# Attention products on all 128 rows: rests of the keys beside zeros, decay and compressed values stacked in parts

## The chip, the cores and the metric

The kernel runs on one core of a Trainium2 chip. The metric is the time of one execution on the device in microseconds. A core has five engines with a queue each: TensorE (PE; its weight loads are shown apart as PEld), VectorE (DVE), ScalarE (ACT), GpSimd (POOL) and SyncE (SP), which issues the transfers.

## The reference

Two blocks of two layers each work on 256 tokens of width 1024 (the first block also on 256 tokens of context). Everything is float32. Cut to what the change touches, in the second block:

```
# forgetting attention: c is the cumulated log of a gate
logits = einsum('bhqd,bhkd->bhqk', q, k) * scale + c[..., q] - c[..., k]
p = softmax(where(k <= q, logits, -inf));  o = p @ v
# compressed, selected and window attention
p_c = masked_softmax(q @ kc + rel, c_end <= t);  o_c = p_c @ vc      # 15 compressed blocks per group
o_s = masked_softmax(q @ k_slc + rel) @ v_slc
o_w = masked_softmax(q @ k_win + rel) @ v_win
out = g0 * o_c + g1 * o_s + g2 * o_w
```

A third attention has a sliding window of 128 with a sink. The first block has two attentions over 512 keys (256 of x and 256 of the context), one of them with a bias per head and one with a window and a sink. Heads have 64 features, and there are 8 heads in each attention.

## The kernel before

Every float32 product is made of products of a faster type. A number is split into a part that this type (float32r) holds exactly and its rest: `mm3` issues part x part, part x rest and rest x part (L546 to L548). Nearly all projections run through it, with weights streamed in chunks of 1024 columns, split by ScalarE (L354) and VectorE (L356; in the first block GpSimd takes every seventh).

For the scores, a head has 64 features, and `stack_q` puts the part of its queries on its own 64 rows and the rest on the other 64, so that one operand of 128 rows holds both. `double_k` puts the keys' part on both halves (`kh`) and the keys' rest on the head's own half (`kl`). A score then is two products: one on 128 rows with `kh`, and one on the head's 64 rows alone with `kl`:

```
PE.matmul(o, qq, kh, start=True, stop=False)                                  # L1659, 128 rows
PE.matmul(o, qq[HEAD[i]], kl[HEAD[i]], start=False, stop=extra is None)       # L1660, 64 rows
```

The same pair stands at L1213 and L1214 (first block, queries of x, 512 keys), L1231 and L1232 (first layer only, queries of the context, 256 keys), and at L1814 and L1819 (second block, 32 compressed and 256 selected keys, and 256 window keys), where z = 0 and z = 1 are the two. L1659 and L1660 serve the sliding window and the forgetting attention. In each attention a unit is a pair of heads j (4 of them) and one head i of the pair, so there are 8 units (16 in the first layer of the first block, half of them the context's), and each has two halves of 128 queries (qt).

The forgetting attention adds the decay of the keys by a third product, L1663: a column of the identity on 8 rows, repeated, times the 8 heads' decays in float32. The compressed values are multiplied by L1869, a float32 product on 30 rows, with `vcmp` and `pc` in float32.

Around them, `soft` computes scores, softmax (L624 adds the bias and takes the maximum, L614 the exponential, L615 to L620 the division); its results are transposed (L1248, L1257, L1684, L1851), split, and multiplied with the values by `mm3`. The projections of the next stage stand in a queue, and `fill(ns)` takes products from it between two steps of an attention. A scheduler then orders all instructions for each engine by its own estimates, with the weights' preparation at a lower priority; memory comes from two arenas in the SBUF (`fa` for float32, `ra` for float32r) whose pieces are given back and reused, so that a writer waits for the last reader of the piece before.

Of the kernel before, what the change touches and what calls it, by code (L numbers as in the profile page):

```python
# [12 lines left out]
F32 = mybir.dt.float32  # L13
# [9 lines left out]
NF = 22            # 2816 / 128 hidden tiles of a feed-forward block  # L23
# [5 lines left out]
CH = 1024          # floats per partition in a weight chunk  # L29

# Column starts of the first block's input projection.
A_GLU, A_GATE, NQ, NK, NV, N_GATE, WQ, WK, WV, W_GATE, MERGE = (
    0, 1024, 1536, 2048, 2560, 3072, 3584, 4096, 4224, 4352, 4864)
# Column starts of the second block's input projection.
# [3 lines left out]
# Heads (j, 4 + j) side by side: the two halves of a 128-row tile then belong to  # L38
# the two key/value groups.
# [4 lines left out]
# --------------------------------------------------------------------------  # L44
# Host: layout only
# --------------------------------------------------------------------------

def chunked(w, cols, ktc):
    """w[K, cols] as chunks [n, 128, ktc * ncols], rows in blocks of 128."""
    w = np.asarray(w)[:, cols]  # L50
    k, n = w.shape
    w = w.reshape(k // (P * ktc), ktc, P, n)
    return np.ascontiguousarray(w.transpose(0, 2, 1, 3)).reshape(-1, P, ktc * n)


def by_tile(w, cols, ktc, width):
    """Column groups of `width`, each as chunks of ktc row blocks."""
# [5 lines left out]
def columns(v):  # L63
    """A vector of n * 128 as [128, n]."""
    return np.asarray(v).reshape(-1, P).T
# [18 lines left out]
def host_arrays(inp):  # L84
# [12 lines left out]
    for l in range(2):  # L97
# [27 lines left out]
        # [h, i, j, r, c] -> rows (i, j), keys (r, c)  # L125
# [5 lines left out]
        # second block  # L131
        w = g["w_in_2"][l]
        for n in (1, 2):
# [7 lines left out]
            np.concatenate([kv(0), kv(1), kv(3), kv(5)]),                 # k_cmp v_cmp v_slc v_win  # L141
            QB + gq,
            np.concatenate([rng(KB, 128), rng(VB, 128), kv(2), kv(4)]),   # k_b v_b k_slc k_win
# [23 lines left out]
    # relative position biases, gathered by distance, masked places padded  # L167
# [17 lines left out]
    # constants that depend on shapes alone  # L185
# [16 lines left out]
    small[[0, 2, 4], 0] = 1.0           # picks and adds the rows of x  # L202
    small[[1, 3, 4], 1] = 1.0           # and of the context
# [8 lines left out]
# --------------------------------------------------------------------------  # L212
# Memory
# --------------------------------------------------------------------------

class Arena:
    """Best-fit allocation inside one SBUF tile. Tile orders the accesses."""
# [62 lines left out]
# --------------------------------------------------------------------------  # L280
# The weight stream
# --------------------------------------------------------------------------

class Weights:
    """Chunks of weights in the order of their use: loaded ahead, each split into a
    part that float32r holds exactly and the rest."""

    NRAW, NHL, NEXTRA, NHLX = 3, 5, 5, 2
    pool = 0           # every so many rests are taken on GpSimd
# [14 lines left out]
    def drop(self):  # L304
        """End of the start, which has more buffers."""
# [6 lines left out]
    def grow(self, n, top=True):  # L312
        """n chunks in parts at a time"""
# [56 lines left out]
    def done(self, i=0):  # L370
        """The oldest of the chunks in use, or one of the others, has been used."""
# [4 lines left out]
class Raws:  # L376
    """Chunks of weights used as they are."""
# [26 lines left out]
# chunks of the conditioning's weights that follow each step of a merge  # L404
# [10 lines left out]
def make_plan(d):  # L415
# [7 lines left out]
    def block1(l):  # L423
# [9 lines left out]
        add(f"tr{l}", 0, 2 * Kern.GLU[l])            # a_glu  # L433
        add(f"nat{l}", 8, 12)
        add(f"tr{l}", 2 * Kern.GLU[l], 8)
        add(f"nat{l}", 12)               # wq, wk wv
        add(f"tr{l}", 8, 20)             # n_gate, some of the merge, w_gate
        add(f"proj{l}", 0, 2)
        for h in range(2, 12):
            if h == 8:  # L440
                add(f"tr{l}", 32, 36)    # a_gate
# [30 lines left out]
# --------------------------------------------------------------------------  # L472
# The kernel
# [1454 lines left out]
```

## Time and profile before

| | |
|---|---|
| median of 3 runs | 2437.91 us (2437.05 to 2439.4) |
| profiled execution, span | 2444.6 us |
| TensorE busy | 2371.6 us, 97% |
| VectorE busy | 1690.7 us, 69% |
| ScalarE busy | 1241.4 us, 51% |
| GpSimd busy | 219.8 us, 9% |
| mean granted clock of TensorE | 0.983 |

The span is that of the one profiled execution, from its first to its last instruction; the profile gives no other time of its own for it. It is 6.7 us above the median of the runs, which carry no profiler. The busy time of TensorE is modelled from pipelined matmuls and says little on how well it is used. What tells more is the distance between the starts of two matmuls that follow one another. The attentions lie at 119 to 355 us and 734 to 870 us (first block, layers 0 and 1) and at 1249 to 1478 us and 1962 to 2188 us (second block).

### The profile page before, as it was taken

How to read it: one execution, taken by the hardware profiler on the slowest of the kernel's cores; microseconds unless marked ns; L12 is line 12 of the kernel's file. 1: busy time of each engine (PE TensorE's matmuls, PEld its weight loads, DVE VectorE, ACT ScalarE, POOL GpSimd, SP SyncE). 2: the span in 40 equal slices, each digit the busy share in tenths (PEclk: the TensorE clock that was granted, in tenths of full speed). 3: DMA queues.
4: the chain of work that ended last, by engine and by line, in shares of the span. 5: the costliest groups of instructions: out<-in, count | busy, mean ns of one | idle time of the engine just before them, and what ended most of it. 6: DMA issues, size and time to landing. Idle time of an engine off the chain costs nothing.

```text
span 2444.6 us, 31998 instructions
## 1 busy us (share of the span) xinstructions
PE 2371.6 (97%) x11660; PEld 1904.4 (78%) x11660; DVE 1690.7 (69%) x3156; ACT 1241.4 (51%) x2201; POOL 219.8 (9%) x223
## 2 busy tenths in 40 slices
PE   6999899999999999999999999999999999999998
PEld 4777777787777899888877777788788777777887
DVE  6588889677688896655667676655655676677554
ACT  6375563232347754444376564444454475654542
POOL 1301200121221112100000000000000000010000
PEclk9999999999999999999999899999999998999999
DMA  8121224455434245556545325556656543425554
GB/s 316 45 69 39 72 70 130 131 165 173 139 103 129 92 135 179 172 183 209 172 143 182 108 82 172 179 191 194 198 177 223 158 164 117 130 93 187 190 188 138
DMA packets 102974, 362.97 MB, mean 148 GB/s; under 512 B 11936, under 2 KB 13088, under 8 KB 102304
## 3 DMA queue, kind: packets, MB, share of 16 engines
q1 hardware_dynamic: 102816, 360.93, 45.2%
q8 instruction: 91, 1.49, 0.2%
q14 instruction: 67, 0.55, 0.1%
HBM read 359.84 MB, written 1.05 MB: 148 GB/s over the span
## 4 chain that ended last, share of the span: by engine, by line
PE 58%; DVE 7%; DMA 3%; ACT 2%; issue 2%; POOL 1%; DVEq 0%; ACTq 0%; POOLq 0%; SPq 0%
PE bank L546 17%; PE bank L548 16%; PE bank L547 16%; DVE ra_t L356 2%; ACT ra_t L354 1%; PE bank L1660 1%; PE bank L1819 1%; PE bank L1385 1%; PE bank L1663 1%; DVE fa_t L851 1%; PE bank L1814 1%; PE bank L1659 1%; DMA fa_t<-in_gate 1%; DMA fa_t<-in_n 1%; DMA fa_t<-in_cw 1%
## 5 line engine op out<-in xcount | busy, mean ns | idle before, releaser
L546 PE MATMUL bank<-ra_t 128*128 128x512 f32 (+1 forms) x3216 | 1193.6, 373 | 12.3 <-DVE fa_t L772 5.0
L548 PE MATMUL bank<-ra_t 128*128 128x512 f32 (+1 forms) x3216 | 1182.6, 369 | 9.8 <-DVE ra_t L536 3.8
L547 PE MATMUL bank<-ra_t 128*128 128x512 f32 (+1 forms) x3216 | 1183.9, 369 | 4.2 <-DVE ra_t L356 2.1
L356 DVE TENSOR_TENSOR ra_t<-fa_t,ra_t 128x1024 fp32r<-128x1024 f32 x583 | 722.2, 1241 | 370.4 <-ACT ra_t L354 354.0
L354 ACT CAST ra_t<-fa_t 128x1024 fp32r<-128x1024 f32 x606 | 632.6, 1047 | 638.7 <-PE bank L548 290.0
L546 PEld LDWEIGHTS bank<-ra_t 128*128 128x128 f32 x3216 | 609.4, 190 | 130.4 <-issue 17.7
L548 PEld LDWEIGHTS bank<-ra_t 128*128 128x128 f32 x3216 | 610.1, 190 | 116.5 <-DVE ra_t L536 7.2
L547 PEld LDWEIGHTS bank<-ra_t 128*128 128x128 f32 x3216 | 610.8, 190 | 107.5 <-issue 5.2
L535 ACT CAST ra_t<-bank 128x512 fp32r<-128x512 f32 (+5 forms) x234 | 112.7, 488 | 116.2 <-PE bank L548 31.1
L536 DVE TENSOR_TENSOR ra_t<-bank,ra_t 128x512 fp32r<-128x512 f32 (+5 forms) x234 | 130.7, 567 | 58.6 <-ACT ra_t L535 56.2
L851 DVE SCALAR_TENSOR_TENSOR fa_t<-fa_t 128x512 f32<-128x512 f32 (+1 forms) x240 | 161.6, 673 | 6.0 <-ACT fa_t L849 2.8
L624 DVE CUSTOM_DVE_ANT_0 fa_t<-bank,fa_t 128x256 f32<-128x256 f32 (+2 forms) x320 | 117.7, 396 | 65.7 <-PE bank L1852 16.3
L542 POOL TENSOR_TENSOR fa_t<-fa_t 128x1 f32<-128x1 f32 (+2 forms) x54 | 68.6, 1271 | 770.0 <-DVE fa_t L541 769.8
L614 ACT ACTIVATE fa_t<-fa_t 128x257 f32<-128x257 f32 (+5 forms) x160 | 91.2, 571 | 31.6 <-DVE fa_t L624 30.8
L1393 ACT ACTIVATE fa_t<-bank 128x256 f32<-128x256 f32 x88 | 33.8, 384 | 114.8 <-PE bank L548 113.5
L356 POOL TENSOR_TENSOR ra_t<-fa_t,ra_t 128x1024 fp32r<-128x1024 f32 x23 | 57.1, 2481 | 302.8 <-ACT ra_t L354 288.1
L1395 DVE TENSOR_TENSOR fa_t<-fa_t,bank 128x256 f32<-128x256 f32 x88 | 36.7, 417 | 67.8 <-ACT fa_t L1393 67.8
L1167 DVE SCALAR_TENSOR_TENSOR fa_t<-fa_t 128x512 f32<-128x512 f32 x98 | 73.2, 778 | 1.9 <-DMA fa_t<-in_ada 1.6
L637 DVE TENSOR_TENSOR ra_t<-bank,ra_t 64x256 fp32r<-64x256 f32 (+1 forms) x96 | 43.5, 455 | 12.9 <-ACT ra_t L636 10.4
L1036 POOL TENSOR_TENSOR fa_t<-fa_t 128x512 f32<-128x512 f32 (+1 forms) x32 | 37.1, 1167 | 154.1 <-DVE fa_t L1035 154.1
L1763 POOL TENSOR_TENSOR fa_t<-fa_t 128x512 f32<-128x512 f32 x8 | 13.9, 1743 | 393.7 <-DVE fa_t L1762 393.7
L1831 ACT ACTIVATE fa_t<-fa_t 128x32 f32<-128x32 f32 (+2 forms) x96 | 38.8, 404 | 17.3 <-DVE fa_t L624 17.0
(211 smaller groups left out, 1746.0 us busy)
## 6 DMA issues: line engine op xcount, KB each, us to landing
fa_t<-in_f1w SPq DMA_DIRECT2D x132, 512.0 KB, 4.2
fa_t<-in_f2w SPq DMA_DIRECT2D x132, 512.0 KB, 4.2
fa_t<-in_tr SPq DMA_DIRECT2D x88, 512.0 KB, 3.6
fa_t<-in_n SPq DMA_DIRECT2D x56, 512.0 KB, 3.9
fa_t<-in_ada SPq DMA_DIRECT2D x48, 512.0 KB, 4.2
fa_t<-in_gate SPq DMA_DIRECT2D x48, 512.0 KB, 3.9
fa_t<-in_nat SPq DMA_DIRECT2D x36, 512.0 KB, 4.4
fa_t<-in_proj SPq DMA_DIRECT2D x24, 512.0 KB, 3.6
```

The lines of the kernel that those rows point to most:

```text
L354: nc.scalar.copy(hi, raw)
L356: eng.tensor_tensor(lo, raw, hi.bitcast(F32), ALU.subtract)
L535: self.nc.scalar.copy(hi, src)
L536: self.nc.vector.tensor_tensor(lo, src, hi.bitcast(F32), ALU.subtract)
L542: self.nc.gpsimd.tensor_tensor(out, out, self.nhalf[:, :n], ALU.pow)
L546: mm(ps, lh, rh, start=start, stop=False)
L547: mm(ps, lh, rl, start=False, stop=False)
L548: mm(ps, ll, rh, start=False, stop=stop)
L614: nc.scalar.activation(s[:, :width or n], s[:, :width or n], AF.Exp, bias=mneg, scale=-1.0, accum_out=r)
L624: self.nc.vector.tensor_tensor_reduce(out=out, in0=a, in1=b, op0=ALU.add, op1=ALU.min, scale=-1.0, scalar=init, accum_out=acc)
L851: V.scalar_tensor_tensor(y4, src, w, y4, ALU.mult, ALU.add)
L1167: V.scalar_tensor_tensor(acc[s].a, wk, self.sc[:, kt, s:s + 1], acc[s].a, ALU.mult, ALU.add)
```

## The change

Every product of the attentions gets 128 rows. `kl` now holds the keys' rest on the head's own half and zeros on the other, and the product with it takes all 128 rows of the queries. The zeros are written once for each buffer by GpSimd (`clear`), 40 times in all: 12 in the first block and 28 in the second, with `ct`, `vcmp` and the two buffers `pc`. The decay becomes float32r: `ct` has the part on rows 0 to 7, the rest on rows 32 to 39 and zeros elsewhere, and `pick` has a one for each head on both. The compressed values are stacked as part, part, rest, and the probabilities as part, rest, part, each 32 rows apart, so that one product of float32r gives the three. That adds one copy on ScalarE and one subtraction on VectorE for each of 32 pieces of 32x128. Comments are gone as well, so lines have other numbers: L546 to L548 are now L547 to L549, L1659, L1660 and L1663 are L1685, L1686 and L1689, L1814 and L1819 are L1847 and L1851, L1869 is L1904, L542 is L543, L1672 is L1698, and L1763 is L1790.

```diff
+    def clear(self, ap):
...
+        self.nc.gpsimd.tensor_copy(ap, self.z1[0:r].to_broadcast([r, n]))
+    def clear_rests(self, ka, kb):
+        self.clear(ka[1][HEAD[1]])
+        self.clear(kb[1][HEAD[0]])
...
+        for k in range(0, 4, 2):
+            self.clear_rests(*((b[:, :512], b[:, 512:]) for b in kr.parts[k:k + 2]))
...
+        self.clear_rests(*wk)
...
-                    PE.matmul(bank, q[HEAD[i], qt * P:qt * P + P], kl[HEAD[i]], start=False, stop=True)
+                    PE.matmul(bank, q[:, qt * P:qt * P + P], kl, start=False, stop=True)
...
-                    PE.matmul(bank[:, qt * 256:qt * 256 + 256], qq[HEAD[i]], kl[HEAD[i], 256:], start=False, stop=True)
+                    PE.matmul(bank[:, qt * 256:qt * 256 + 256], qq, kl[:, 256:], start=False, stop=True)
...
-        ct = fa.alloc(S)
+        ct, pickb = ra.alloc(S), ra.alloc(8)
+        pick = pickb.a
+        self.clear(ct.a)
+        G.tensor_tensor(pick, ident[:, 0:8], ident[:, 32:40], ALU.add)
...
+            V.scalar_tensor_tensor(ct.a[32:40], bank[0:8, :S], -1.0, ct.a[0:8].bitcast(F32), ALU.mult, ALU.subtract)
...
-        vcmp = fa.alloc(P)
+        vcmp = ra.alloc(P)
+        self.clear(vcmp.a)
...
+                A.copy(vcmp.a[32:62], bank[0:30, 0:P])
+                V.tensor_tensor(vcmp.a[64:94], bank[0:30, 0:P], vcmp.a[0:30].bitcast(F32), ALU.subtract)
...
-                    PE.matmul(o, qq[HEAD[i]], kl[HEAD[i]], start=False, stop=extra is None)
+                    PE.matmul(o, qq, kl, start=False, stop=extra is None)
...
-                        PE.matmul(bank[:, qt * P:qt * P + n], ident[0:8, h:h + 1].to_broadcast([8, P]), extra[:, 0:n],
+                        PE.matmul(bank[:, qt * P:qt * P + n], pick[:, h:h + 1].to_broadcast([P, P]), extra[:, 0:n],
...
+        self.clear_rests(*kws)
...
+        self.clear_rests(*ksl)
+        self.clear_rests(*kwi)
...
-        pcr = Ring(fa, S, 2)
+        pcr = Ring(ra, S, 2)
+        self.clear(pcr.parts[0])
+        self.clear(pcr.parts[1])
...
-                    rows_ = HEAD[i] if z else slice(0, P)
-                    PE.matmul(bs[:, 160 * qt:160 * qt + W1], q[rows_, qt * P:qt * P + P], sl4[rows_, i, z],
+                    PE.matmul(bs[:, 160 * qt:160 * qt + W1], q[:, qt * P:qt * P + P], sl4[:, i, z],
...
-                A.copy(pc[0:32, k * P:k * P + P], bank[0:32, 384:512])
+                cq, bq = slice(k * P, k * P + P), bank[0:32, 384:512]
+                A.copy(pc[0:32, cq], bq)
+                V.tensor_tensor(pc[32:64, cq], bq, pc[0:32, cq].bitcast(F32), ALU.subtract)
+                A.copy(pc[64:96, cq], bq)
...
-            PE.matmul(o, vcmp.a[0:30], pc[0:30], start=False, stop=True)
+            PE.matmul(o, vcmp.a, pc, start=False, stop=True)
```

On TensorE, the first unit of the forgetting attention in layer 0, before. A row has its number, its line, the operation, what it writes and reads, and the size that it writes.

```order
6063 L548 MATMUL bank_63<-ra_t 128x512
6064 L1659 MATMUL bank_66<-ra_t 128x256
6065 L1660 MATMUL bank_66<-ra_t 128x256
6066 L1663 MATMUL bank_66<-fa_t 128x128
6067 L1659 MATMUL bank_66<-ra_t 128x256
6068 L1660 MATMUL bank_66<-ra_t 128x256
6069 L1663 MATMUL bank_66<-fa_t 128x256
6070 L546 MATMUL bank_63<-ra_t 128x512
```

The same unit now:

```order
6070 L547 MATMUL bank_63<-ra_t 128x512
6071 L1685 MATMUL bank_66<-ra_t 128x256
6072 L1686 MATMUL bank_66<-ra_t 128x256
6073 L1689 MATMUL bank_66<-ra_t 128x128
6074 L1685 MATMUL bank_66<-ra_t 128x256
6075 L1686 MATMUL bank_66<-ra_t 128x256
6076 L1689 MATMUL bank_66<-ra_t 128x256
6077 L548 MATMUL bank_63<-ra_t 128x512
```

The six products stand together in both, in the same order; the decay's now read float32r (`ra_t`).

On GpSimd, the second block's first layer, before. L1672 copies a head's sink beside its scores, L542 is the power in a norm, and L1763 adds a branch's output.

```order
106 L356 TENSOR_TENSOR ra_t<-fa_t,ra_t 128x1024
107 L1672 COPY fa_t<-fa_t 128x1 x4
108 L542 TENSOR_TENSOR fa_t<-fa_t 128x1 x2
109 L1672 COPY fa_t<-fa_t 128x1 x12
110 L1763 TENSOR_TENSOR fa_t<-fa_t 128x512 x4
```

The same stretch now, where L649 is a clear:

```order
116 L1698 COPY fa_t<-fa_t 128x1 x4
117 L649 CAST ra_t<-fa_t 64x256
118 L543 TENSOR_TENSOR fa_t<-fa_t 128x1
119 L649 CAST ra_t<-fa_t 64x256
120 L543 TENSOR_TENSOR fa_t<-fa_t 128x1
121 L1698 COPY fa_t<-fa_t 128x1 x10
122 L649 CAST ra_t<-fa_t 64x256
123 L1698 COPY fa_t<-fa_t 128x1 x2
124 L649 CAST ra_t<-fa_t 64x256 x6
125 L649 CAST ra_t<-fa_t 128x256 x2
126 L649 CAST ra_t<-fa_t 64x256
127 L1790 TENSOR_TENSOR fa_t<-fa_t 128x512 x4
```

A clear now stands ahead of each of the two powers, one ahead of the last two sinks, and nine ahead of the branch's additions.

## Rows read from the trace of the kernel before

**Rows 1.** The page: busy time by engine, and the clock granted in 40 slices.

```profile
PE 2371.6 (97%) x11660; PEld 1904.4 (78%) x11660; DVE 1690.7 (69%) x3156; ACT 1241.4 (51%) x2201; POOL 219.8 (9%) x223
...
PEclk9999999999999999999999899999999998999999
```

**Rows 2.** Waits of TensorE: who waited for whom, us in total, times, longest.

```profile
PE bank L1129 <- ACT ra_t L354: 14.4, 1, 14.4
...
PE bank L1248 <- DVE fa_t L620: 0.4, 1, 0.4
```

**Rows 3.** Timeline of TensorE, sliding window: start, us, line, operands, rows*columns, shape.

```profile
1255.41 0.28 PE L1659 MATMUL bank<-ra_t 128*128 128x256 f32 x1
1255.62 0.38 PE L1660 MATMUL bank<-ra_t 64*128 64x256 f32 x1
1255.93 0.39 PE L1659 MATMUL bank<-ra_t 128*128 128x256 f32 x1
...
1256.78 0.40 PE L547 MATMUL bank<-ra_t 128*128 128x512 f32 x1
...
1257.71 0.28 PE L546 MATMUL bank<-ra_t 128*128 128x256 f32 x1
1257.83 0.28 PE L547 MATMUL bank<-ra_t 128*128 128x256 f32 x1
```

**Rows 4.** Timeline of TensorE, first block, 512 keys.

```profile
122.21 0.39 PE L547 MATMUL bank<-ra_t 128*128 128x512 f32 x1
122.44 0.39 PE L1213 MATMUL bank<-ra_t 128*128 128x512 f32 x1
...
124.37 0.39 PE L546 MATMUL bank<-ra_t 128*128 128x512 f32 x1
```

**Rows 5.** Timeline of TensorE, a unit of the forgetting attention in layer 1.

```profile
2076.81 0.28 PE L1659 MATMUL bank<-ra_t 128*128 128x256 f32 x1
2077.02 0.38 PE L1660 MATMUL bank<-ra_t 64*128 64x256 f32 x1
2077.33 0.48 PE L1663 MATMUL bank<-fa_t 8*128 8x128 f32 x2
...
2078.36 0.69 PE L1663 MATMUL bank<-fa_t 8*128 8x256 f32 x2
2078.99 0.64 PE L546 MATMUL bank<-ra_t 128*128 128x512 f32 x1
```

**Rows 6.** Timeline of TensorE, compressed values of one unit.

```profile
1413.71 0.69 PE L1869 MATMUL bank<-fa_t 30*128 30x256 f32 x2
...
1414.67 0.40 PE L548 MATMUL bank<-ra_t 128*128 128x512 f32 x1
```

**Rows 7.** TensorE's groups by shape: count, busy us, mean ns, idle before.

```profile
L1214 PE MATMUL bank<-ra_t 64*128 64x512 f32 x64 | 32.0, 501 | 0.0
...
L1660 PE MATMUL bank<-ra_t 64*128 64x256 f32 x64 | 25.4, 396 | 0.0
...
L1663 PE MATMUL bank<-fa_t 8*128 8x256 f32 x32 | 13.5, 508 | 0.0
```

**Rows 8.** Windows: length, busy us of PE, PEld, DVE, ACT, POOL, clock, DMA, GB/s.

```profile
119.00:217.00 98.00, 97.55 (x507) 74.71 (x506) 82.50 (x214) 70.47 (x147) 2.59 (x2) 1.00 0.22 68
...
267.00:355.00 88.00, 87.45 (x449) 66.71 (x447) 76.08 (x205) 61.75 (x133) 10.55 (x28) 1.00 0.18 59
...
870.00:930.00 60.00, 59.99 (x504) 59.63 (x503) 57.29 (x99) 28.71 (x46) 10.90 (x7) 1.00 0.45 142
...
1322.00:1367.00 45.00, 45.00 (x184) 31.49 (x185) 29.89 (x100) 24.84 (x67) 0.00 (x0) 0.83 0.21 67
...
1401.00:1478.00 77.00, 76.96 (x365) 57.30 (x366) 56.69 (x215) 47.78 (x156) 5.68 (x3) 0.96 0.29 96
```

**Rows 9.** Groups by shape on ScalarE and GpSimd.

```profile
L1854 ACT COPY fa_t<-bank 32x128 f32<-32x128 f32 x32 | 7.6, 248 | 2.1 <-DVE ra_t L536 1.7
...
L887 POOL TENSOR_TENSOR fa_t<-fa_t 128x512 f32<-128x512 f32 x2 | 3.9, 1960 | 1.6 <-DVE fa_t L772 1.6
```

More of the change, by code (lines that the diff above doesn't have):

```diff
@@ L518, in __init__ @@
         nc.vector.memset(z, 0.0)
-        self.zero = z[:, 0:1].to_broadcast([P, 256])
+        self.z1 = z[:, 0:1]
+        self.zero = self.z1.to_broadcast([P, 256])
     def const(self, key):
@@ L640, in hi_lo @@
             nc.vector.scalar_tensor_tensor(lo, src, sc, hi.bitcast(F32), ALU.mult, ALU.subtract)
+    def clear(self, ap):
+        n = 1
+        for m in ap.shape[1:]:
+            n *= m
+        assert len(ap.shape) == 2
+        r = ap.shape[0]
+        self.nc.gpsimd.tensor_copy(ap, self.z1[0:r].to_broadcast([r, n]))
+    def clear_rests(self, ka, kb):
+        self.clear(ka[1][HEAD[1]])
+        self.clear(kb[1][HEAD[0]])
     def double_k(self, bank, ka, kb, n, sc=None):
@@ L1769, in mix @@
         kr = Ring(ra, 2 * S, 4)
+        for k in range(0, 4, 2):
+            self.clear_rests(*((b[:, :S], b[:, S:]) for b in kr.parts[k:k + 2]))
         f3 = self.fm.a[:, 512:768]
@@ L1778, in mix @@
         ogc, og_c = new_og()
-        simple(prep_c, vch, vcl, True, og_c, ct.a[0:8])
+        simple(prep_c, vch, vcl, True, og_c, ct.a)
         self.flush()
-        for b in (kr, vcb, qcb, kcb, ogb, ct):
+        for b in (kr, vcb, qcb, kcb, ogb, ct, pickb):
             b.free()
@@ L1817, in soft @@
                 for z in range(2):
-                    rows_ = HEAD[i] if z else slice(0, P)
-                    PE.matmul(bw[:, P * qt:P * qt + S], q[rows_, qt * P:qt * P + P], wi4[rows_, i, z],
+                    PE.matmul(bw[:, P * qt:P * qt + S], q[:, qt * P:qt * P + P], wi4[:, i, z],
                               start=z == 0, stop=z == 1)
```

## Prediction

> **What bounds the kernel now.** I read the shares of the page first. TensorE is busy 97% of the span, VectorE 69%, ScalarE 51%, GpSimd 9%, and the granted clock is at or near full in every slice but for two that read 8 [rows 1]. Then I asked whom TensorE waits for: the longest wait is one of 14.4 us in the start, and the list, which falls in length, has 0.4 us in all for a softmax's division (L620) [rows 2]. So TensorE sets the pace, the attentions included. But a busy share does not tell what it is busy with, so I read starts of matmuls in the timeline. Plain products of 256 columns start 0.12 us apart (1257.71 to 1257.83), while an attention's set of two products on 128 rows and two on 64 rows takes from 1255.41 to 1256.78, with one more product of 256 columns behind it [rows 3]. Five products at 0.12 us would be 0.60 us; they take 1.37 us. The set changes its number of rows four times (128 to 64, back, to 64, back), so each change costs (1.37 - 0.60) / 4 = 0.19 us. With 512 columns the plain step is 0.23 us (122.21 to 122.44), and the set and one more product take 1.93 us (122.44 to 124.37) where five steps are 1.15 us: 0.78 us for four changes [rows 4]. The price is the same at both widths, so it hangs on the change of rows and not on the work.
>
> The Trainium skill, in "TensorEngine Tiling (Array Packing)", section Key Properties, says that a change of tiling mode drains the engine. The trace agrees, at 0.19 us a change. The page gives no price, so by the page alone the sum would be a count of changes; by the rows it is the sum below.
>
> **What the change removes.** Per layer the units are 4 pairs of heads x 2, and both layers together give these sets.
>
> First block, queries of x against 512 keys: 64 products on 64 rows [rows 7], so 32 sets x 0.78 us = 25.0 us. Queries of the context in the first layer, 256 keys (L1232): by the loop 32 products on 64 rows, 16 sets x 0.77 = 12.3 us. Of the 64 products of L1660 [rows 7] half belong to the second block's sliding window: 16 sets x 0.77 = 12.3 us. Compressed, selected and window attention: by the loops of L1814 and L1819 64 products on 64 rows, 128 changes x 0.19 = 24.3 us.
>
> Forgetting attention: the other half of L1660, with the decay behind each product. The decay is a float32 product on 8 rows, which the profile records as two instructions (32 records of 256 columns for 16 products) [rows 7]. One unit's six products take from 2076.81 to 2078.99, 2.18 us [rows 5]. Afterwards they are six single products on 128 rows, at most 0.12 us each, 0.72 us. The saving is 1.46 us x 16 units = 23.4 us. Compressed values: a float32 product on 30 rows, again two records; from 1413.71 to the second product behind it, 1414.67, are 0.96 us [rows 6], afterwards 0.12 + 0.23 = 0.35 us. That is 0.61 x 16 = 9.8 us.
>
> The sum is 25.0 + 12.3 + 12.3 + 24.3 + 23.4 + 9.8 = **107 us of TensorE's path**. The streaming of columns is not made dearer: the products on 64 rows already stream the same columns.
>
> **Clock.** The granted clock is 0.83 between 1322 and 1367 us, the forgetting attention [rows 8], where the changes stand closest and most products have 8 rows. That is (1 - 0.83) x 45 = 7.7 us of lost clock in a layer, 15 us in both. What the profile does not show is whether fuller products keep the clock at 2.4 GHz: the gain is between 0 and 15 us. I take 4 us, because VectorE then becomes the limit of that stage: it is busy 29.9 of the 45 us [rows 8], and TensorE without the changes needs 45 - 8 x 1.46 = 33.3 us, so only some 2 us a layer can be used.
>
> **What takes part of it back.** VectorE can be kept busy 57.29 of 60 us, 95.5%, where TensorE is full too [rows 8]; this I take as its ceiling. Between 119 and 217 us TensorE loses 8 sets x 0.78 + 8 x 0.77 = 12.4 us and needs 85.6; VectorE needs 82.50 / 0.955 = 86.4: 0.8 us back. Between 267 and 355 us 88 - 12.4 = 75.6 stands against 76.08 / 0.955 = 79.7: 4.1 us back. Between 1401 and 1478 us TensorE goes to 77 - 8 units x (8 changes x 0.19 + 0.61) = 60 us; VectorE has 56.69 us and gets 16 new subtractions of 32x128. The trace has none of that shape on VectorE; ScalarE's copy of that shape takes 248 ns [rows 9], a subtraction of nothing would be the lower end and a 128x512 one on GpSimd, 1960 ns [rows 9], the far upper one; I take 0.3 us, near the row of the same shape. So (56.69 + 4.8) / 0.955 = 64.4 us: 4.4 us back in each layer, 9 in both. Together 14 us. ScalarE's 16 additional copies x 0.248 = 4 us a layer I count at nothing: it is busy 47.78 of the 77 us, and even of 64 us 52 leave room.
>
> **GpSimd's 40 clears** (12 in the first block, 28 in the second) have no row of their own kind; nothing is the lower bound, and 1.96 us for 128x512 the upper: at most 78 us spread over a span in which GpSimd is busy 220 us [rows 1, 9]. They cost the path nothing as long as the memory they clear is free before the keys come; the work that hides them is the projection ahead of each attention. If that cover is gone, what is queued behind them are the sinks' copies and the powers of the norms, and ScalarE's exponential waits for the first and VectorE for the second. The order shows clears ahead of two such powers in each layer of the second block. I count 0; a us or two each would be 4 to 8 us.
>
> **Order.** On TensorE the first block's order is the same as before. In the second block the scheduler puts fillings elsewhere: in the compressed stage more of them stand between a unit's scores and its own transposes (in seven of a layer's eight units), so a softmax has more cover there and not less. In the forgetting attention each unit's six products stay together, as before. On SP's queue some loads of the gates, of their biases and of a norm's vectors change places in the stage of the branches; no weight is loaded twice and none later than a buffer frees. Both I count at nothing; without cover the price would be that of rival 1.
>
> **The sum.** 107 - 14 + 4 = 97 us. It is made against the profiled execution, whose span is 2444.6 us; the median of the timed runs is 2437.91 us, 6.7 us less, and nothing in the sum scales with that. 2438 - 97 = **2341 us**.
>
> **Rivals.**
> 1. *Half of it.* VectorE and ScalarE answer each other in softmax (reduction, exponential, reciprocal, division), and in-order queues reach 95% only where no such chain runs. If they lose half of the gain in every stage but the forgetting one, the saving is 55 to 80 us: 2358 to 2383. For it speaks that VectorE stands at 82.5 of 98 us already [rows 8]; against it, that it idles there for TensorE's products, which come earlier.
> 2. *VectorE is the bound.* It stays at today's share in the first block (nothing gained of 37 us) and in the compressed stage (nothing of 34): what is left is 23 + 12 = 36 us, 2402. Against it: TensorE never waits for the division now.
> 3. *The change doesn't do what it says.* The 0.31 us between 64 and 128 rows could come from accumulating into the same bank or from fetching new weights. Then only the float32 products' second instructions go, at half of a pair each (2078.36 to 2078.99 [rows 5]): 16 x 3 x 0.32 = 15 us, 2423. Against it: plain triples also accumulate in one bank with new weights, 0.12 us apart [rows 3].
> 4. *Half rows are cheaper rows.* If a product on 64 rows took half of the array and its neighbour the other half, filling the rows would add half a plain step for each: 160 x 0.06 + 64 x 0.115 = 17 us (160 products of 256 or 288 columns, 64 of 512), and with the 15 us of rival 3 the time would be 2440. The Trainium skill's "TensorEngine Tiling (Array Packing)", section Theoretical Speedup, gives up to 2x for a contraction of at most 64 rows. The trace does not agree here: no product starts beside another, a change back to 128 rows or on to 8 takes 0.31 us [rows 3, 5].
> 5. *Slower.* GpSimd's queue is the place: a clear waits until TensorE has read the last user of its memory, and a norm's power or a sink stands behind it, so that softmax or the next projection starts late. It decides from 97 / 40 = 2.4 us of standing still for each clear; at 3 us each the kernel takes 2341 + 120 = 2461.
>
> **How the numbers follow.** The forecast (80 to 122 us saved) has 69 in 100, rival 1 has 13, rival 2 has 8, rival 3 has 3, rival 4 has 2 and rival 5 has 5. The range holds the forecast and rival 1, 82 in 100: its lower end is 107 us and all 15 us of clock, without any loss to VectorE, 2438 - 122 = 2316; its upper end 2383. A change of under 0.2%, 5 us, is about what a measurement of this kernel cannot tell from none; only rival 4 lies there. Faster 0.93, same 0.02, slower 0.05.
>
> **What will show it.** In the timeline of the changed kernel the products of a set start 0.12 us apart (0.23 with 512 columns) with no step of 0.31 us left; L1663's successor is one record instead of two; the first attention's window shrinks from 98 to about 87 us, the compressed one from 77 to about 64, with VectorE busy over 90% in both; the granted clock of the forgetting attention rises above 0.83. Wrong would be: steps of 0.3 us that remain on full rows (rival 3), long waits of TensorE for divisions on VectorE (rivals 1 and 2), or waits whose releaser is a clear on GpSimd (rival 5).

## The result, and the profile after

The changed kernel takes 2343.26 us (median of 4 runs, 2342.75 to 2346.41), the kernel before takes 2438.65 us beside it (4 runs, 2437.05 to 2440.54). The ratio is 0.9613, 95% interval 0.96 to 0.9627, so 95.4 us are gone. The profiled execution has a span of 2344.6 us, 100.0 us less than that of before. Its page, the shares of the engines and the granted clock, in the form of [rows 1]:

```profile
PE 2261.1 (96%) x11612; PEld 1858.8 (79%) x11612; DVE 1696.6 (72%) x3192; ACT 1249.1 (53%) x2235; POOL 244.0 (10%) x265
...
PEclk9999999999999999999999999999999999999999
```

TensorE is busy 110.5 us less than before and idle 10.5 us more; VectorE and ScalarE have hardly more to do. The two slices with an 8 are gone.

The timeline of TensorE, first a set with 512 columns, which answers to [rows 4], then one with 256 columns in the sliding window [rows 3]:

```profile
121.73 0.40 PE L1230 MATMUL bank<-ra_t 128*128 128x512 f32 x1
121.97 0.40 PE L1231 MATMUL bank<-ra_t 128*128 128x512 f32 x1
122.20 0.39 PE L549 MATMUL bank<-ra_t 128*128 128x512 f32 x1
...
1226.92 0.27 PE L1685 MATMUL bank<-ra_t 128*128 128x256 f32 x1
1227.03 0.28 PE L1686 MATMUL bank<-ra_t 128*128 128x256 f32 x1
1227.15 0.28 PE L1685 MATMUL bank<-ra_t 128*128 128x256 f32 x1
1227.27 0.28 PE L1686 MATMUL bank<-ra_t 128*128 128x256 f32 x1
```

The rests' products (L1231, L1686) start one plain step behind the parts': 0.23 us with 512 columns, 0.12 with 256. A unit of the forgetting attention [rows 5], and the compressed values of a unit (L1904) [rows 6]:

```profile
1293.62 0.36 PE L1685 MATMUL bank<-ra_t 128*128 128x256 f32 x1
1293.83 0.28 PE L1686 MATMUL bank<-ra_t 128*128 128x256 f32 x1
1293.94 0.22 PE L1689 MATMUL bank<-ra_t 128*128 128x128 f32 x1
1294.00 0.33 PE L1685 MATMUL bank<-ra_t 128*128 128x256 f32 x1
...
1294.41 0.40 PE L547 MATMUL bank<-ra_t 128*128 128x512 f32 x1
...
1362.36 0.28 PE L1904 MATMUL bank<-ra_t 128*128 128x256 f32 x1
1362.48 0.73 PE L1847 MATMUL bank<-ra_t 128*128 128x288 f32 x4
```

The unit takes 0.79 us (1293.62 to 1294.41) where it took 2.18, and the decay (L1689) is one record with a step of 0.06 us for 128 columns. The compressed values take 0.12 us.

The windows of the stages, cut more exactly than in [rows 8] (length, busy us of PE, PEld, DVE, ACT and POOL, granted clock, share of the DMA engines, GB/s). First the kernel before, cut at each stage's first and last matmul: first attention, forgetting and compressed stage of layer 0, the same two of layer 1; then the changed kernel, in the same order:

```profile
118.50:216.70 98.20, 97.71 (x507) 74.75 (x506) 82.97 (x215) 70.66 (x146) 2.59 (x2) 1.00 0.22 68
1321.50:1374.10 52.60, 52.60 (x211) 37.71 (x211) 33.12 (x109) 28.03 (x74) 0.00 (x0) 0.81 0.18 59
1400.60:1477.50 76.90, 76.86 (x366) 57.34 (x365) 56.35 (x215) 48.01 (x156) 5.68 (x3) 0.96 0.29 95
2034.20:2085.40 51.20, 51.20 (x211) 36.76 (x211) 33.12 (x109) 28.03 (x74) 0.00 (x0) 0.83 0.20 64
2111.90:2187.40 75.50, 75.46 (x366) 56.20 (x365) 56.32 (x215) 47.96 (x156) 5.67 (x3) 0.98 0.30 96
```

```profile
118.20:207.20 89.00, 87.32 (x506) 73.04 (x507) 82.86 (x215) 69.81 (x145) 5.66 (x4) 1.00 0.23 75
1291.50:1329.70 38.20, 37.12 (x213) 29.39 (x213) 35.37 (x112) 30.25 (x76) 1.86 (x5) 1.00 0.39 127
1350.80:1424.20 73.40, 70.66 (x404) 57.40 (x403) 67.33 (x236) 55.54 (x176) 6.15 (x4) 1.00 0.36 117
1966.10:2004.30 38.20, 37.13 (x213) 29.43 (x213) 35.41 (x112) 30.28 (x76) 1.86 (x5) 1.00 0.39 126
2025.30:2098.80 73.50, 70.71 (x404) 57.51 (x403) 67.34 (x236) 55.59 (x176) 6.16 (x4) 1.00 0.37 117
```

The reader is to see two things. The forgetting stage is shorter by 14.4 and 13.0 us, and its clock stands at full speed. The compressed stage is shorter by only 3.5 and 2.0 us, but it now holds 404 matmuls instead of 366: fillings moved into it, and the stretch behind it fell from 81.0 to 69.3 us and from 80.4 to 69.0. A stage's length alone therefore says little here.

So I cut TensorE's time in the trace differently. Each step from one matmul's start to the next is divided into its plain length (0.228 us for 512 columns, 0.116 for 256, 0.131 for 288, 0.060 for 128; 0.215 and 0.109 for a float32 record of 256 and 128 columns), half of what it spent at 1.2 GHz, and the excess. The excess is put to "changes of rows" where the two matmuls have different numbers of rows, to "step behind a change" where they have the same number and the step before was a change, and to "other" elsewhere. The second belongs to the price of a change, as e7 shows below: in the kernel before, 187 such steps have an excess of 0.107 us in the middle. These are my own sums over all steps of the two profiled executions:

| us | before | after | difference |
|---|---|---|---|
| plain length | 2151.8 | 2139.3 | -12.5 |
| changes of rows | 91.8 (532 changes) | 5.3 (20) | -86.5 |
| step behind a change | 18.7 (187) | 1.8 (20) | -16.9 |
| clock at 1.2 GHz | 39.3 | 15.4 | -23.9 |
| other excess | 120.1 | 160.2 | +40.1 |
| sum | 2421.7 | 2322.0 | -99.7 |

A change thus costs (86.5 + 16.9) / 512 = 0.20 us. The other excess grew only where changes were removed: from 4.3 to 7.9 us in the first attention of the first block, 2.8 to 6.1 in its second, 10.9 to 15.2 in the layer-1 attention, and in each layer of the second block from 2.0 to 4.6 in the sliding window, 1.3 to 5.7 in the forgetting and some 1.8 to 9.1 in the compressed stage. TensorE's weight loads show what it consists of. Waits of the weight loads in the compressed stage of layer 0 after the change (waiting line, releaser, us in total, times, longest):

```profile
PEld bank L1883 <- DVE fa_t L1872: 4.3, 6, 1.3
PEld bank L547 <- ACT ra_t L536: 2.1, 7, 0.4
PEld bank L1904 <- ACT ra_t L1889: 1.5, 5, 0.5
PEld bank L548 <- DVE ra_t L537: 0.8, 3, 0.4
PEld bank L547 <- ACT fa_t L1863: 0.6, 1, 0.6
...
```

The transposes now wait for softmax's divisions (L1872), values for the parts of the probabilities (L536, L537), and the compressed values for the last of the copies that the change added (L1889). The same list of before has 0.4 us for such a part, 0.3 for a division (L1840) ahead of a score and not of a transpose, and nothing for a copy.

A wait costs more than itself, as a stretch of the second attention shows: first the timeline of TensorE, then the one wait of a weight load within it.

```profile
276.02 0.40 PE L1231 MATMUL bank<-ra_t 128*128 128x512 f32 x1
276.36 0.39 PE L547 MATMUL bank<-ra_t 128*128 128x256 f32 x1
276.59 0.39 PE L548 MATMUL bank<-ra_t 128*128 128x512 f32 x1
```

```profile
PEld bank L547 <- ACT ra_t L536: 0.4, 1, 0.4
```

The step onto the late product (L547) takes 0.34 us instead of 0.23, and the step behind it, of 256 columns, 0.23 instead of 0.12. Of the growth of 40 us, steps onto a product that waited for another engine's result hold 25, and the steps behind them 9 (my own sums over the stages listed above, by the releasers that the profile infers).

### The profile page after: what moved, and what is told of

Its sections match the earlier page's. It is cut to its first block, busy times and chain, and to the rows that moved or that the text cites. A ratio compares the mean times of both kernels' runs of the same rounds, so it can differ in the third digit from the quotient of the medians.

```text
span 2344.6 us, 32027 instructions
## 1 busy us (share of the span) xinstructions
PE 2261.1 (96%) x11612; PEld 1858.8 (79%) x11612; DVE 1696.6 (72%) x3192; ACT 1249.1 (53%) x2235; POOL 244.0 (10%) x265
## 4 chain that ended last, share of the span: by engine, by line
PE 55%; DVE 8%; ACT 4%; DMA 3%; issue 2%; POOL 1%; DVEq 0%; ACTq 0%; POOLq 0%; SPq 0%
PE bank L547 17%; PE bank L549 17%; PE bank L548 16%; DVE ra_t L356 2%; ACT ra_t L354 1%; DMA fa_t<-in_gate 1%; PE bank L1402 1%; DVE ra_t L537 1%; DVE fa_t L625 1%; DVE fa_t L1339 1%; DMA fa_t<-in_n 1%; PE bank L1265 1%; ACT ra_t L536 1%; POOL fa_t L543 0%; ACT fa_t L1863 0%
## 5 line engine op out<-in xcount | busy, mean ns | idle before, releaser
L547 PE MATMUL bank<-ra_t 128*128 128x512 f32 (+1 forms) x3216 | 1186.9, 371 | 14.3 <-DVE fa_t L786 5.0
L549 PE MATMUL bank<-ra_t 128*128 128x512 f32 (+1 forms) x3216 | 1172.8, 366 | 8.3 <-DVE ra_t L537 3.8
L548 PE MATMUL bank<-ra_t 128*128 128x512 f32 (+1 forms) x3216 | 1174.6, 367 | 3.8 <-DVE ra_t L537 1.3
L547 PEld LDWEIGHTS bank<-ra_t 128*128 128x128 f32 x3216 | 605.4, 189 | 129.1 <-ACT ra_t L536 15.4
L549 PEld LDWEIGHTS bank<-ra_t 128*128 128x128 f32 x3216 | 605.6, 189 | 108.7 <-DVE ra_t L537 7.3
L548 PEld LDWEIGHTS bank<-ra_t 128*128 128x128 f32 x3216 | 607.2, 189 | 103.1 <-DVE ra_t L356 5.1
L537 DVE TENSOR_TENSOR ra_t<-bank,ra_t 128x512 fp32r<-128x512 f32 (+5 forms) x234 | 131.2, 568 | 44.0 <-ACT ra_t L536 41.1
L536 ACT CAST ra_t<-bank 128x512 fp32r<-128x512 f32 (+5 forms) x234 | 112.8, 488 | 84.8 <-PE bank L549 33.4
L543 POOL TENSOR_TENSOR fa_t<-fa_t 128x1 f32<-128x1 f32 (+2 forms) x54 | 69.0, 1278 | 762.3 <-DVE fa_t L542 762.1
L649 POOL CAST ra_t<-fa_t 64x256 fp32r<-64x256 f32 (+3 forms) x40 | 24.0, 606 | 241.4 <-PE bank L1597 69.9
L1863 ACT ACTIVATE fa_t<-fa_t 128x32 f32<-128x32 f32 (+2 forms) x96 | 39.0, 409 | 14.5 <-DVE fa_t L625 13.9
```

The source lines that it names most:

```text
L536: self.nc.scalar.copy(hi, src)
L537: self.nc.vector.tensor_tensor(lo, src, hi.bitcast(F32), ALU.subtract)
L543: self.nc.gpsimd.tensor_tensor(out, out, self.nhalf[:, :n], ALU.pow)
L547: mm(ps, lh, rh, start=start, stop=False)
L548: mm(ps, lh, rl, start=False, stop=False)
L549: mm(ps, ll, rh, start=False, stop=stop)
```

## Experiments

**One half of the change each.** e1_rests: the changed kernel, but the decay and the compressed values stay float32 on 8 and 30 rows.

```diff
-        vcmp = ra.alloc(P)
+        vcmp = fa.alloc(P)
...
-                        PE.matmul(bank[:, qt * P:qt * P + n], pick[:, h:h + 1].to_broadcast([P, P]), extra[:, 0:n],
+                        PE.matmul(bank[:, qt * P:qt * P + n], ident[0:8, h:h + 1].to_broadcast([8, P]), extra[:, 0:n],
...
-            PE.matmul(o, vcmp.a, pc, start=False, stop=True)
+            PE.matmul(o, vcmp.a[0:30], pc[0:30], start=False, stop=True)
```

> The changed kernel with one half of the change alone: the keys' rests stand beside zeros and take 128 rows, while the decay (8 rows) and the compressed values (30 rows) stay float32 products as before. My theory (a change of the number of rows costs TensorE 0.19 us, and VectorE gives a part of it back): 25.0 + 12.3 + 12.3 + 24.3 us of the sum, and in the forgetting attention 4 changes instead of 6 a unit, 16 x 2 x 0.19 = 6 us, so 80 us less the 14 us that VectorE takes back: 66 us, 2372 us. The clock: if the products on 8 rows are what lowers it, it stays near 0.85 in the forgetting attention; if the changes between 64 and 128 rows do, it rises. The rival, that only the float32 products' second instructions go away, expects no gain here, 2438 us.

e2_parts: the changed kernel, but the keys' rests are taken on 64 rows as before, and nothing is cleared for them.

```diff
-                    PE.matmul(bank, q[:, qt * P:qt * P + P], kl, start=False, stop=True)
+                    PE.matmul(bank, q[HEAD[i], qt * P:qt * P + P], kl[HEAD[i]], start=False, stop=True)
...
-                    PE.matmul(o, qq, kl, start=False, stop=extra is None)
+                    PE.matmul(o, qq[HEAD[i]], kl[HEAD[i]], start=False, stop=extra is None)
```

> The other half alone: decay and compressed values stacked as parts and rests on 128 rows in float32r, while the keys' rests stay on 64 rows. My theory: a unit of the forgetting attention goes from 2.18 us to six steps of 0.12 and four changes of 0.19, 1.48 us, 16 x 0.70 = 11 us, and the compressed values bring their 9.8 us: 21 us, 2417 us, and up to 15 us more if the clock comes back with the products on 8 rows gone. If the changes lower the clock, nothing more. Both halves together should make up the whole change, 95 us, but for what the clock and VectorE's ceiling make not additive.

Measured: e1 2361.8 us, ratio 0.9681 (0.9663 to 0.9699); e2 2410.5 us, ratio 0.9872 (0.9857 to 0.9887). Of 2440 us that is 78 and 31, together 109, while the whole change gives 94 (0.9613). Some 15 us are thus counted twice. e1 came out 10 us below its expectation, whose sum had no clock in it. The windows of the forgetting stage show what is counted twice; of e1, then of e2, both layers:

```profile
1287.90:1328.50 40.60, 40.60 (x211) 30.31 (x211) 32.67 (x108) 27.83 (x74) 0.78 (x2) 1.00 0.24 79
1970.00:2010.70 40.70, 40.70 (x213) 30.39 (x212) 32.72 (x109) 27.93 (x74) 0.78 (x2) 1.00 0.25 82
```

```profile
1326.40:1368.60 42.20, 42.12 (x214) 31.86 (x214) 35.60 (x112) 30.28 (x76) 0.80 (x2) 1.00 0.37 115
2018.00:2060.20 42.20, 42.11 (x213) 31.83 (x213) 35.58 (x112) 30.30 (x76) 0.80 (x2) 1.00 0.37 115
```

The clock of this stage was 0.81 and 0.83; it is 1.00 with either half of the change. Either half brings it back alone, so both runs hold its 18.7 us, and the 4.6 us of the compressed stages, where neither trace has a stretch at 1.2 GHz. Against that, 416 changes go in e1 and 64 in e2, 32 fewer than the 512 together, which is 6 us at 0.20: 17 us in all.

**Fewer changes, same products.** e3_grouped: the kernel before, where the two products on 128 rows of a unit of 512 keys stand ahead of the two on 64 rows. In the program 40 of the 532 changes go (492 are left in the trace).

```diff
-                    PE.matmul(bank, q[HEAD[i], qt * P:qt * P + P], kl[HEAD[i]], start=False, stop=True)
                     bk.append(bank)
+                for qt in range(2):
+                    PE.matmul(bk[qt], q[HEAD[i], qt * P:qt * P + P], kl[HEAD[i]], start=False, stop=True)
```

> The kernel before with one edit in the first block: of each unit on 512 keys first both products on 128 rows, then both on 64 rows. Nothing is filled with zeros and every product stays as it is. As the scheduler orders it, TensorE changes between 128 and 64 rows 88 times there instead of 128. My theory: 40 x 0.19 = 7.8 us less on TensorE's path, of which 5 to 8 us show in the time, so 2431 to 2433 us, and in the timeline a product on 64 rows starts 0.23 us after another one on 64 rows. The rival, that a product on 64 rows is slow by itself (its own weights, or its adding to the bank just written), expects no change of the time and 0.4 us between all starts at products on 64 rows.

Measured: 2431.97 us (11 runs), ratio 0.997 (0.9958 to 0.9981), 7.3 us less (4.6 to 10.2). Forty changes at 0.20 us are 8 us. No row was filled, no zeros were multiplied: the change of rows itself has the price.

**Products on 64 rows in a row.** e7_all64: the kernel before, where the first product of a set also has 64 rows; the part of the scores from the queries' rests is left out.

```diff
-                    PE.matmul(bank, q[:, qt * P:qt * P + P], kh, start=True, stop=False)
+                    PE.matmul(bank, q[HEAD[i], qt * P:qt * P + P], kh[HEAD[i]], start=True, stop=False)
```

> The kernel before with the first block's products on 512 keys on 64 rows both, the first one too: the part of the scores that comes from the queries' rests is left out. One look at the timeline. My theory: two products on 64 rows that follow one another start 0.23 us apart, like two on 128 rows, and a change costs 0.19 us more wherever it stands. The rival, that 64 rows are slow by themselves: 0.4 us between them as well.

Measured: 2438.39 us (one run, which lies within the spread of the kernel before, 2438.09 to 2447.18). The timeline of TensorE around one unit:

```profile
121.09 0.40 PE L547 MATMUL bank<-ra_t 128*128 128x512 f32 x1
121.42 0.50 PE L1213 MATMUL bank<-ra_t 64*128 64x512 f32 x1
121.76 0.39 PE L1214 MATMUL bank<-ra_t 64*128 64x512 f32 x1
121.99 0.39 PE L1213 MATMUL bank<-ra_t 64*128 64x512 f32 x1
122.22 0.39 PE L1214 MATMUL bank<-ra_t 64*128 64x512 f32 x1
122.54 0.50 PE L548 MATMUL bank<-ra_t 128*128 128x512 f32 x1
122.88 0.39 PE L546 MATMUL bank<-ra_t 128*128 128x512 f32 x1
```

Products on 64 rows behind one another start 0.23 us apart, as those on 128 rows do. The excess lies only at the edges: 0.10 us in the step onto the other number of rows, and 0.11 in the step behind that. The Trainium skill, "TensorEngine Tiling (Array Packing)", section Key Properties, says that a change of mode drains the engine. The trace agrees in that it has a stall at each change, and adds its price, 0.2 us in two steps. Half rows in a row are neither cheaper nor dearer than full ones here, against rival 4. Both products of a set lie on the same half, though; what two products on different halves would do, no run shows.

**GpSimd's clears.** e4_clears2: the changed kernel with every clear written twice.

```diff
+        for _ in range(2):
-        self.nc.gpsimd.tensor_copy(ap, self.z1[0:r].to_broadcast([r, n]))
+            self.nc.gpsimd.tensor_copy(ap, self.z1[0:r].to_broadcast([r, n]))
```

> The changed kernel with every one of GpSimd's 40 clears made twice. My theory: the clears are off the path, hidden behind the projections, so the time is that of the changed kernel, 2343 us, within 3 us. The rival, that a clear holds GpSimd's queue and with it norms and sinks: the clears' 24 us of GpSimd again, in part or whole, so up to 2367 us.

Measured: 2346.48 us, ratio 0.9612 (0.96 to 0.9625), against 0.9613 for the changed kernel. The groups of clears in the changed kernel (shape and count, busy us and mean ns, idle before):

```profile
L649 POOL CAST ra_t<-fa_t 64x256 fp32r<-64x256 f32 x20 | 10.2, 510 | 159.3 <-PE bank L1597 69.9 <-DVE fa_t L616 34.3 <-PE bank L1685 34.1
L649 POOL CAST ra_t<-fa_t 64x512 fp32r<-64x512 f32 x12 | 8.9, 738 | 67.2 <-PE bank L1249 48.0 <-PE bank L548 11.3 <-PE bank L1231 3.5
```

A clear takes 0.5 to 0.7 us on an engine that is busy 10% of the span, and 40 more of them cost nothing.

**VectorE's load in the first block.** e5_before_noconv and e6_after_noconv: the kernel before and the changed one, with 30 of the convolution's 31 taps left out, which fill VectorE beside the attentions of the first block.

```diff
-            for k in range(31):
+            for k in range(1):
```

> The kernel before with 30 of the 31 taps of the first block's convolution left out: some 232 instructions of 0.67 us on VectorE, 156 us, which run beside both attentions and the merges of that block. It is the other kernel's reference. TensorE's work is that of the kernel before. I expect little: TensorE seldom waits for VectorE there, so 2420 to 2438 us.

> The changed kernel with the same 30 taps left out. My theory: in the first block 27 of 37 us showed, and the other 10 went to VectorE, which is near full there. Without the taps VectorE has room, so the first block gives nearly its whole 37 us: this kernel is 103 to 106 us below the kernel before without the taps, where the change with the taps brought 95. The rival, that it is the latency of each unit's softmax (VectorE and ScalarE in turn) and not VectorE's load: the difference stays at 95 us.

Measured: 2433.19 us, ratio 0.9953 (0.9938 to 0.9967), and 2337.16 us, ratio 0.9564 (0.9548 to 0.958). The change gives 96.0 us between the two, not the 103 to 106 of the theory. The window of the first attention of e6:

```profile
117.30:206.20 88.90, 87.36 (x506) 73.73 (x507) 62.82 (x185) 74.94 (x153) 4.23 (x4) 1.00 0.23 75
```

VectorE is busy 62.82 us where it was 82.86, 71% of the window instead of 93%, and the stage takes 88.9 us as it did (89.0). VectorE's load does not hold it.

**The divisions.** e8_divs: the changed kernel with a third of the compressed stage's divisions, and half of those of the second block's other attentions, on ScalarE.

```diff
-            for s, r in todo:
-                V.tensor_scalar(s, s, r, None, ALU.mult)
+            for k, (s, r) in enumerate(todo):
+                if k % 3 == 1:
+                    A.mul(s, s, r)
+                else:
+                    V.tensor_scalar(s, s, r, None, ALU.mult)
...
-        self.W.pool, self.share = 0, False
+        self.W.pool, self.share = 0, True
```

> The changed kernel, with VectorE relieved of divisions in the second block only: two of the six divisions of a unit in the compressed, selected and window attention, and every second one in the sliding window and the forgetting attention, stand on ScalarE. In the profile of the changed kernel TensorE's matmuls and weight loads wait 2.2 and 4.3 us for these divisions in one compressed stage, and 0.8 and 2.4 us in one forgetting stage. Theory A (what took part of the gain back in the second block is the load and the queue of VectorE, whose six divisions take 2.4 us in a row): these waits shrink and the kernel gains 3 to 8 us, 2335 to 2340. Theory B (what is missing is cover: the softmax chain as a whole, with its hops between engines, is longer than the work that TensorE now has behind the scores): ScalarE's division comes behind its exponentials and adds a hop, and the time stays within 3 us of the changed kernel, 2341 to 2347.

e9_cover: the changed kernel with more filling ahead of a unit's transposes.

```diff
-            self.fill(2500)
+            self.fill(3500)
...
-            self.fill(1000)
+            self.fill(0)
```

> The changed kernel with the same work, and more of the filling placed between a unit's scores and its own transposes instead of behind its values: the planner's budgets ahead of the transposes go from 1500 to 2200 in the first block, from 1300 to 1900 in the sliding window and the forgetting attention, from 2500 to 3500 in the compressed one, and those behind the values from 700, 700 and 1000 to 0, 100 and 0. Theory B (cover): TensorE's small waits for divisions go, 23 us of the steps between matmuls are in play, and the kernel gains 3 to 12 us, 2331 to 2340; what could eat it is that the next unit's scores then follow the values at once and the parts of the probabilities (L536, L537) are waited for more. Theory A (VectorE's load): the order of TensorE's work changes nothing that VectorE has to do, no gain, 2341 to 2347.

e10_after_again, the base of the two:

> The changed kernel once more, on the same chip as the two with fewer divisions on VectorE and with more cover, as their base: 2343 to 2346, 0.961 of the kernel before.

Measured: e8 ratio 0.9601 (0.9586 to 0.9615), e9 0.9622 (0.9605 to 0.9639), e10 0.9604 (0.9589 to 0.9619); one execution of e9 took 7231.71 us and is not in its ratio. Neither gains; the median of e9, 2351.57 us, lies above the ranges of both theories. In e8 the waits of the weight loads in the compressed stage only changed their names:

```profile
PEld bank L547 <- ACT ra_t L536: 2.9, 6, 0.7
PEld bank L1907 <- ACT ra_t L1892: 1.9, 5, 0.5
PEld bank L1886 <- ACT fa_t L1873: 1.6, 6, 0.5
PEld bank L1887 <- DVE fa_t L1875: 1.2, 1, 1.2
...
```

They sum to 9.8 us in the whole list, against 10.0 in the changed kernel. Theory A, VectorE's queue, is not borne out. e9 doesn't decide on theory B: in the compressed stage its plain length and its other excess came out as they were (64.2 and 9.0 us), so that the larger budget moved nothing there; in the first block fillings changed places and nothing was gained; in the forgetting stage the weight loads' waits for the division (L621) fell from 2.4 to 1.3 us and the stage's other excess from 5.7 to 5.4.

e11_after_nodiv and e12_before_nodiv: the changed kernel and the one before, with the softmax divisions of the second block left out.

```diff
-            for s, r in todo:
-                V.tensor_scalar(s, s, r, None, ALU.mult)
...
-        else:
+        elif self.W.pool:
```

> The changed kernel without the softmax divisions of the second block (the six of a unit in the compressed, selected and window attention, and those of the sliding window and the forgetting attention, are left out; reductions, exponentials and reciprocals stay). Between the two traces TensorE's steps outside the changes of rows and the clock grew by 23 us in all, some 16 us of them in these stages of the second block: in the compressed stage from 4.2 to 9.0 us, in the forgetting one from 3.6 to 5.7, in the sliding window from 2.9 to 4.7, in each layer. Theory A (TensorE now waits for the end of the softmax chain, which the changes used to cover): with the last link gone the waits go, 4 to 10 us less than the changed kernel, 2335 to 2341. Rival C (what grew belongs to TensorE's own steps: weight loads of products that have short neighbours now, and waits for the parts of the probabilities behind the transposes, which stay as they are): within 3 us of the changed kernel, 2342 to 2348.

> The kernel before without the same divisions of the second block. TensorE waited 0.4 us in all for a division there, so I expect no change: 0.998 to 1.002 of the kernel before. The difference to the changed kernel without them is what the change gives when no division can be waited for: 100 us or more by theory A, 95 to 97 by rival C.

Measured: e11 2336.98 us, ratio 0.9572 (0.9558 to 0.9585); e12 2434.54 us, ratio 0.9982 (0.9966 to 0.9998). Against e10 the changed kernel gains 0.32% without them, some 8 us. Its other excess, with the steps behind a change, falls from 162.0 to 155.8 us (a second profile of the changed kernel, e10, is 2.2 us above the first): from 9.0 to 6.2 in the compressed stage, from 5.7 to 5.4 in the forgetting one, and not at all in the sliding window (4.7 to 4.6). In e12 it fell by 2.0 us, and its executions happened to have a higher granted clock (0.988 in the middle, against 0.986 for before, which is 5 us). Between e12 and e11 lie 97.6 us, which is between what the two theories gave (100 or more, 95 to 97) and decides nothing. So the end of the softmax chain is 6 of the 40 us. What holds the rest in the compressed stage is seen in e11's waits of the weight loads there:

```profile
PEld bank L1902 <- ACT ra_t L1887: 2.1, 4, 0.7
PEld bank L1659 <- ACT ra_t L1887: 1.8, 3, 0.9
PEld bank L547 <- ACT ra_t L536: 0.6, 1, 0.6
...
```

L1887 is there the copy that the change added, L1902 the product of the compressed values, and L1659 the first work behind a pair.

## Why the prediction came out right, and where its terms were off

The forecast was 2341 us and the measurement 2343.26, but the sum is nearer than its terms: three of them missed by 9, 20 and 26 us, and the three errors happened to cancel. The mechanism of the largest term was right; that the number came out so near is luck.

**The price of a change and its count: right, the size 9 us too small.** Changes and second float32 records were put at 107 us; they measure 86.5 + 16.9 + 12.5 = 115.9. The mechanism is shown by e3, where only the order of the same products changes, and by e7. The price is nearly the same in all stages: with the step behind a change it is 0.21 us in the first attention of the first block (12.8 us for 62 changes), 0.20 in the compressed stage (15.6 for 79) and 0.19 in the forgetting one (9.1 for 48), each without what the clock adds. Part of what is missing was left out of the rows: the unit of the forgetting attention [rows 5] was read up to the start of the product behind it, without the step behind its last change, and the compressed values [rows 6] from their own start, without the step onto them.

**The clock, the first step that failed: some 24 us instead of 4.** I held a return of the clock to be worth 4 us, "because VectorE then becomes the limit of that stage". It gave 18.7 us in the forgetting stages ((1 - 0.81) x 52.6 + (1 - 0.83) x 51.2) and 4.6 in the compressed ones (0.04 x 76.9 + 0.02 x 75.5), which I had not counted. My upper bound of 15 us came from a window of 45 us which left out the end of a stage of 52.6. VectorE did not stop it: with fillings in it, it is busy 35.37 of 38.2 us, 93%. Nor do most products of the stage have 8 rows, as the prediction says: 32 of its 211 records do. The clocks of the other executions say the same: those of before have a granted clock of 0.986 in the middle (17 runs beside e11), the four of the changed kernel 0.993 to 0.996, so 0.014 x 2440 = 34 us against some 13. The scatter of before goes with it: its fastest of those 17, 2432.89 us, had 0.990, its slowest, 2452.62 us, had 0.982, and 0.008 x 2440 is 19.5 us of the 19.7 between them. The profiled execution of before had 0.983, so its span lies above the median, and the two profiles differ by 100 us where the medians differ by 95. Why the clock falls in this stage stays open.

**What was taken back, the second: 40 us instead of 14, and mostly not for the reason given.** My ceiling of 95.5% for VectorE gave 0.8 and 4.1 us in the first block; the growth there was 3.7 and 3.3, and 4.3 in layer 1, and e6 shows that the first stage is no shorter at 71%. For the compressed stages I had 9 us and 14.7 came, as waits for single results: 2.8 us in layer 0 for the divisions (e11), some 1.5 for the copies L1889, which I had counted at nothing by ScalarE's share. I had nothing for the sliding window and the forgetting stage, where 13.9 us came. That the changes had covered short waits of this kind is what all of these stages have in common; the trace puts 34 of the 40 us to such waits and the steps behind them, e11 shows for 6 us that they go when their cause goes, and for the rest that is argued and not shown. Rival 1, the chain of softmax, named the mechanism, at 17 to 42 us beyond my sum; it came to 26 us beyond it. By this term alone the time would have lain in that rival's range; the clock and the price of a change made up for it.

**GpSimd's clears at nothing: right**, by e4, and no list of waits names one as releaser. **Order at nothing: right in the sum**, though fillings of some 11 us moved between the compressed stage and the stretch behind it, so that the compressed window did not shrink to the 64 us that I gave as a sign. **Rivals 2 and 4** fall by the time itself (2402 and 2440 us against 2343), **rivals 3 and 5** by e3 and by e4.

## What to carry to other kernels

Before counting how full a matmul is, read the distance between starts where its shape differs from its neighbours': here a product on half the rows cost as much as a full one, and each change between the two cost 0.20 us more, so that filling with zeros, or only grouping equal shapes (e3), was worth it. When a stall of the busiest engine is removed, list what it waited out: the results that came just in time then come late, by a few tenths of a microsecond each, and here more than a quarter of what was removed went there (40 of 140 us). And when a forecast comes out, check its terms one by one: here three errors hid in a sum that came out right. A granted clock below full in a stage belongs into the sum at its whole length, since it can come back with any one of the causes removed.

## What the runs showed of the hardware that was not expected

The clock of the forgetting stage rose from 0.81 to 1.00 when only its changes between 128 and 64 rows went (e1, the products on 8 rows still there), and also when only the products on 8 rows went (e2). And the price of a change is split: e7 shows 0.10 us ahead of the first matmul with the new number of rows and 0.11 us behind it, whichever way the change goes (121.09 to 121.76, and 122.22 to 122.88). The second half is not special to a change: a product whose weight load waited for a result is followed by the same step, 0.11 us longer (276.36 to 276.59).
